# Attention scores of a hybrid transformer layer: the low parts of the queries on 128 rows

## The chip, the cores and the metric

One Trainium2 chip, one core. The metric is the time of one execution in microseconds on the device, the median of the runs. Engines are named as in the profile: PE is TensorE (PEld its weight loads), DVE is VectorE, ACT is ScalarE, POOL is GpSimd, SP issues DMAs.

## What is computed

One layer of a diffusion backbone in float32, for 512 latent tokens and 128 prompt tokens with the same weights: a modulated norm, one input projection to pooling channels, queries, keys, values and gates, a pooling mixer, a differential attention, gates and output projection, and a feed-forward part. The part that the change touches is the attention. Per head (8 of them) there are two maps m of 64 features; the latent queries read 640 keys (128 cached, 512 own), the prompt's queries read the 128 prompt keys:

```
def block(qi):
    s = jnp.einsum('bqhmd,bkhmd->bhmqk', qi, k).astype(jnp.float32) * scale
    p = jax.nn.softmax(s, axis=-1)
    a = p[:, :, 0] - lam * p[:, :, 1]
    return jnp.einsum('bhqk,bkhe->bqhe', a, vf)
```

## The kernel before

TensorE multiplies in a float32 format with a shortened mantissa. To keep the accuracy, every operand is split into a high part (the rounded value) and a low part (the rest), and a product is the sum of high x high, high x low and low x high, accumulated in PSUM. `mm` (L141) issues each of these products; all have line L142 in the profile, transposes L145.

The kernel runs in stages: startup (norm, modulation, the first head's projections), attention from about 78 to 382 us, pooling mixer and gates, output projection, feed-forward. In the attention the order on TensorE is written out by hand: `PHASES` (L465) has one string of steps per head, and `pin` (L136) keeps the program's order on TensorE. The order on VectorE, ScalarE and POOL is the planner's, which runs its own timing of the program (L1192). The steps are:

- `S`tm: `attend` (L651), scores of query tile t, map m: four products into one PSUM buffer `s`, then the maximum (`nm`, VectorE, L667), the exponential (`p`, ScalarE, L669), and after map 1 the scaled difference of both maps. For t = 4, the prompt's, both maps come at once with 128 keys each.
- `x`: `between` (L580), transposes of the cached keys of the next head and the prompt's new keys (`mx`), and sums of squares.
- `T`, `P`: `turned` (L679) transposes the differences (`pat`), `values` (L701) multiplies them with the values (`po`).
- `p`, `b`: one step of the projections that run between: queries (`psq`), keys (`psk`), values (`psv`), pooling channels (`psu`).

`s`, `pat` and `mx` share two PSUM buffers (`bankS`, L97), so the third of them in a row waits until the first one's readers are done.

The two maps lie on partitions 0 to 63 and 64 to 127. `k_split` writes, per map, a tile of 128 rows `ks`: the keys' high parts on the map's own rows, their low parts on the other 64. `q_part` (L552) writes, per map, `qd` with the queries' high part on both halves, and one tile `ql` for both maps with the low parts, each map's on its own rows (L562, VectorE); `ql` has two buffers, for the heads in turn. A score is then two products (`scores`, L645): `qd` with all 128 rows of `ks` (high x high and high x low at once), and the map's 64 rows of `ql` with its 64 rows of `ks` (low x high). The rotation of queries and keys (`rope`) runs on ScalarE, VectorE and POOL (L541), and POOL issues the stores of the new keys (L596) and values (L639).

The program is made in L1184 with the default size of the scratch that POOL's DMAs use, 16384 bytes per partition.

Of the kernel before, what the change touches and what calls it, by code (L numbers as in the profile page):

```python
# [12 lines left out]
F32R = mybir.dt.float32r  # L13
# [5 lines left out]
P = 128  # L19
# [48 lines left out]
def trunk_kernel(ctx: ExitStack, tc: tile.TileContext, a: dict, o: list):  # L68
# [46 lines left out]

    # ---------------------------------------------------------------- weights
    def wload(src, shape, name, eng=nc.vector):
        """src: DRAM AP of the tile's shape [P, a, b]; returns its exact (hi, lo) parts."""
        n = shape[0] * shape[1]
        raw = wpool.tile([P, 1024], F32, tag="raw", name=f"raw_{name}", bufs=3)  # L120
        rv = raw[:, :n]
        nc.sync.dma_start(rv.rearrange("p (a b) -> p a b", a=shape[0]), src)
        hi = wpool.tile([P, 1024], F32R, tag="whi", name=f"whi_{name}")
        lo = wpool.tile([P, 1024], F32R, tag="wlo", name=f"wlo_{name}")
        nc.scalar.copy(hi[:, :n], rv)  # L125
        eng.tensor_tensor(lo[:, :n], rv, f(hi[:, :n]), ALU.subtract)  # L126
        return (hi[:, :n].rearrange("p (a b) -> p a b", a=shape[0]),
                lo[:, :n].rearrange("p (a b) -> p a b", a=shape[0]))
# [7 lines left out]
    def pin(ins):  # L136
        """While pinned, the order on TensorE is the program's."""
        if pinned[0]:
            tc.keep_in_program_order(ins)
# [12 lines left out]
    def proj(ps, w, act, nk, c0=0, halves=(0, 1)):  # L152
        """ps[128 features, 640 tokens] = w[:, :, c0:c0+128]^T act, for these halves of the tokens."""
        (wh, wl), (ah, al) = w, act
        for k in range(nk):
            for i, (s, m) in enumerate(((wh, ah), (wh, al), (wl, ah))):
                for b in halves:
                    mm(ps[:, b, :HALF], s[:, k, c0:c0 + P], m[:, k, b * HALF:(b + 1) * HALF],
                       k == 0 and i == 0, k == nk - 1 and i == 2)
# [10 lines left out]

    # -------------------------------------------------------------- constants
    ident = const.tile([P, P], F32, tag="ident", name="ident")
# [20 lines left out]

    # ------------------------------------------------------------ modulation
    def put_shift(dst, ps, js):
# [12 lines left out]
    def ada_acc(pool, col, hf, name):  # L208
        """Generator: acc[p, cond, n] = sum over k of silu(c)[cond, k, p] * w_ada[k, p, col + n], with b_ada
        on partition 0, so that the sum over partitions is the modulation row."""  # L210
        c0 = col + hf * 512
# [20 lines left out]
    def acc_rows(acc, i, ps):  # L232
        """The rows of both conditions as rows 2 i and 2 i + 1 of ps[8, 512], i = 0 ... 3."""
        for n, x in enumerate(acc_split(acc, f"n2{i}")):
            for c in range(2):
                r = 2 * i + c
                mm(ps[:8, :], onerow[:, 7 - r:15 - r], x[:, c, :], i + n + c == 0, i + n + c == 5)

    def rows_cols(pool, ps):
        """Their columns: rows 0-3 are the shifts of norm 2 (two halves, two conditions), rows 4-7 the scales."""  # L240
        rows = pool.tile([8, 512], F32, tag="n2rows", name="n2rows", bufs=1)
# [11 lines left out]
    def acc_bcast(acc, dst, cols, name):  # L253
        """dst[c][128, cols] = the row on all partitions."""
        hi, lo = acc_split(acc, name)
# [13 lines left out]

    # ---------------------------------------------------------------- startup  # L270
    with tc.tile_pool(name="boot", bufs=1, reuse_waits="tile") as boot:
# [33 lines left out]
        def w_load(i):  # L305
            """Input rows i * 512 ... of the first head's q and k columns (0, 1); the second head's q columns (2)."""
            raw = wraw[i] = wpool.tile([P, 1024], F32, tag="raw", name=f"raw_first{i}", bufs=3)
# [76 lines left out]
        def ada_sum(i):  # L384
            """w_ada as the moving operand: in two exact parts, or (the first chunk) in float32 passes."""
            i, u = divmod(i, 10)
# [45 lines left out]
        def part(j, k):  # L432
            """Input rows k * 128 ... of the first head's queries (0), its keys (1), the second head's queries (2)."""
            if k == 0:
# [15 lines left out]

    # -------------------------------------------------------------- attention
    oraw = res.tile([P, NH, TOK], F32, tag="r2", name="oraw")
# [52 lines left out]
    with tc.tile_pool(name="att", bufs=2, reuse_waits="tile") as att:  # L505
# [4 lines left out]
        def cache_load(kind, i):  # L510
            """Cached keys or values of heads 2i and 2i + 1."""
            src, dst, n = {"ck": (cache_k, CK, 2), "cv": (cache_v, CV, 1)}[kind]
            dst[i] = att.tile([P, 256], F32, tag=kind, name=f"{kind}{i}", bufs=n)
            nc.sync.dma_start(dst[i], src[:, i * 256:(i + 1) * 256])
# [19 lines left out]
        def rope(ps, name, scale):  # L534
            """The positions' turn of the latent tokens, and a power of two as scale."""
            sh = att.tile([P, TOK], F32, tag="rsh", name=f"rsh_{name}")[:, :LAT]
# [15 lines left out]
        def q_part(h, ps=None, bank=bankP):  # L552
# [5 lines left out]
            qd = [att.tile([P, TOK], F32R, tag=f"qd{m}", name=f"qd{m}_{h}") for m in range(2)]  # L558
            ql = att.tile([P, TOK], F32R, tag="ql", name=f"ql{h}")
            for r, o, t in MAPS(qd):  # L560
                nc.scalar.copy(t[r], y[r])
                nc.vector.tensor_tensor(ql[r], y[r], f(t[r]), ALU.subtract)  # L562
                nc.gpsimd.tensor_copy(t[o], f(t[r]))
            Q[h] = qd, ql

        def MAPS(pair):
            """Per map: its rows, the others, its tile."""
            lo, hi = slice(0, HD), slice(HD, P)
# [5 lines left out]
        def k_split(h, y, cols):  # L574
            """High parts on the map's own rows, low parts on the others."""
            for r, o, t in MAPS(K[h]):
# [3 lines left out]
        def between(h, bank=bankS):  # L580
            """Cached keys of head h + 1, the prompt's new keys of head h, sums of squares of head h - 2: row r
            (tokens below HALF) and row 32 + r (the others) of ssq are head r's."""
            ps = bank(f"mx{h}")
# [61 lines left out]
        def scores(out, h, m, q0, k0, n):  # L645
            qd, ql = Q[h]
            r, _, k = MAPS(K[h])[m]
            mm(out, qd[m][:, q0:q0 + P], k[:, k0:k0 + n], True, False)
            mm(out, ql[r, q0:q0 + P], k[r, k0:k0 + n], False, True)

        def attend(h, t, m):  # L651
            """Map m of one query tile (t == 4: the prompt's, both maps); at the end, p0 / z0 - lam * p1 / z1."""
            name = f"{h}{t}"
# [25 lines left out]
        def turned(h, i):  # L679
            """The differences of key tiles 2i and 2i + 1, keys on partitions."""  # L680
            k0 = 2 * i
# [19 lines left out]
        def values(h, i):  # L701
            """Key tiles 2i and 2i + 1 of head h; the last call ends the head."""
            vh, vl = V[h // 2]
# [37 lines left out]
        def u_pool(g):  # L741
            """In place: the windows' means minus u itself, at u's own columns."""
            u = U[g]
# [28 lines left out]
        def weights(kind, i):  # L772
            """The weights of this step; those of the next one start to load."""
            n = need.index((kind, i))
# [11 lines left out]
        def project(b, n):  # L786
            """n steps of the projections that stand by."""
            while n:
# [5 lines left out]
        def step(h, op):  # L794
# [13 lines left out]
            else:  # L808
                between(NH + 1 if kind == "z" else h)

        W["q", 1] = FIRST[2]
        weights("q", 1)
# [29 lines left out]

    # ------------------------------------- pooling mixer, gates, merged branch
    with ExitStack() as mctx:
# [121 lines left out]

    # --------------------------------------------- output projection, norm 2
    h2 = mg
# [4 lines left out]
    def ffn_half(i, u):  # L973
        """Activation (u = 0) or gate tile i for the first half of the tokens; its PSUM tile and weights."""
        w = wcols(w_fi, u * FF + i * P, P, 0, KD, f"f{'au'[u]}{i}")
# [15 lines left out]
    with tc.tile_pool(name="wo", bufs=1, reuse_waits="tile") as wo:  # L991
# [16 lines left out]
        def out_steps(t):  # L1008
            """The output projection of tile t, then its residual and norm; yields after every second k."""
            ts = slice(t * P, (t + 1) * P)  # L1010
# [52 lines left out]

    # -------------------------------------------------------------------- ffn
    actx.close()
# [31 lines left out]
    def finish(t, pieces):  # L1097
        """The last columns of x2[t], from these PSUM pieces, and its norm: columns 0 to 511 are times fw already."""
        zs, c0 = [], 512
# [96 lines left out]
```

## Time and profile before

| | us |
|---|---|
| time, median of 3 runs | 1147.55 |
| lowest and highest | 1144.93, 1147.86 |
| profiled execution: span from the first to the last instruction | 1142.9 |
| profiled execution: TensorE busy | 1118.8 |
| profiled execution: VectorE busy | 695.0 |

The profiled execution has no time of its own beside the span; the table's median takes in what lies before the first instruction and after the last. An engine is counted as busy from an instruction's start to its end; products on TensorE overlap, so that their pace is read from the distance of their starts, not from their durations. An idle time that ended in "issue" is one in which the engine waited for nothing that the profile shows.

### The profile page before, as it was taken

The numbers are of one execution on the slowest core, as the hardware profiler recorded it, in microseconds if no ns is written. First come the engines' busy times: TensorE is split into PE (matmuls) and PEld (weight loads), VectorE is DVE, ScalarE is ACT, GpSimd is POOL, SyncE is SP. The second block draws the span as 40 slices with busy tenths as digits, with TensorE's granted clock in tenths as the row PEclk, the third lists the DMA queues.
The fourth block names the chain that finished last, engine by engine and source line by source line (L and its number), as shares of the span: only waits on it lengthen the run. The fifth ranks groups of instructions, "written<-read, shape, count | busy, mean of one in ns | idle before, by whom it ended". The sixth has DMA issues, their size and how long they took to land.

```text
span 1142.9 us, 16737 instructions
## 1 busy us (share of the span) xinstructions
PE 1118.8 (98%) x6811; PEld 1013.6 (89%) x6811; DVE 695.0 (61%) x1041; ACT 488.5 (43%) x783; POOL 158.6 (14%) x156
## 2 busy tenths in 40 slices
PE   6989999999999999999999999999999999999997
PEld 4778888888888999999999889999988899999886
DVE  5977767767775667787775658565424344444254
ACT  8746656656655454223233434333321133333123
POOL 3444223133121263000000000000000000000020
PEclk9989999999999999999999999999999999999999
DMA  9821112102101113446457105333222322222212
GB/s 310 234 72 60 48 30 63 38 26 80 38 23 41 37 56 117 142 149 184 149 164 238 60 19 148 91 113 92 73 85 69 89 74 75 74 75 78 70 38 92
DMA packets 128478, 106.10 MB, mean 93 GB/s; under 512 B 4173, under 2 KB 110205, under 8 KB 128402
## 3 DMA queue, kind: packets, MB, share of 16 engines
q1 hardware_dynamic: 126450, 101.93, 29.1%
q0 software_dynamic: 1232, 1.80, 0.7%
q8 instruction: 53, 0.87, 0.3%
q10 hardware_dynamic: 720, 1.31, 0.3%
q14 instruction: 23, 0.19, 0.1%
HBM read 101.36 MB, written 3.67 MB: 92 GB/s over the span
## 4 chain that ended last, share of the span: by engine, by line
PE 92%; DVE 3%; ACT 1%; SPq 1%; issue 1%; DMA 1%; ACTq 0%; DVEq 0%
PE pfa L142 13%; PE pfu L142 13%; PE acc L142 12%; PE ps_g L142 10%; PE s L142 7%; PE psyb L142 5%; PE psk L142 5%; PE pso L142 5%; PE psv L142 5%; PE psq L142 4%; PE psu L142 3%; PE po L142 3%; PE psya L142 2%; PE pat L145 2%; DMA araw_sh<-in_w_ada_dram 1%
## 5 line engine op out<-in xcount | busy, mean ns | idle before, releaser
L142 PE MATMUL pfu<-mg,whi_fu 128*128 128x320 f32 x704 | 134.1, 309 | 0.0
L142 PE MATMUL pfa<-mg,whi_fa 128*128 128x320 f32 x704 | 134.1, 309 | 0.0
L142 PEld LDWEIGHTS pfa<-mg,whi_fa 128*128 128x128 f32 x704 | 111.0, 188 | 0.4
L142 PEld LDWEIGHTS pfu<-mg,whi_fu 128*128 128x128 f32 x704 | 110.8, 188 | 0.0
L142 PE MATMUL acc<-whi_fo,gA 128*128 128x512 f32 (+1 forms) x336 | 101.0, 380 | 0.0
L142 PE MATMUL ps_g<-hT,whi_g 128*128 128x320 f32 x512 | 96.7, 311 | 0.0
L667 DVE TENSOR_REDUCE nm<-s 128x1 f32<-128x640 f32 (+1 forms) x80 | 57.2, 715 | 51.3 <-PE s L142 50.2
L669 ACT ACTIVATE p<-s,nm 128x640 f32<-128x640 f32 (+1 forms) x80 | 56.7, 709 | 61.0 <-DVE nm L667 60.4
L142 PE MATMUL pfa<-mg,wlo_fa 128*128 128x320 f32 x352 | 82.2, 307 | 0.0
L142 PE MATMUL pfu<-mg,wlo_fu 128*128 128x320 f32 x352 | 82.2, 307 | 0.0
L142 PEld LDWEIGHTS ps_g<-hT,whi_g 128*128 128x128 f32 x512 | 80.2, 188 | 2.0 <-issue 1.5
L126 DVE TENSOR_TENSOR wlo_fo<-raw_fo,whi_fo 128x1024 fp32r<-128x1024 f32 (+1 forms) x24 | 27.3, 1144 | 80.8 <-ACT whi_fo L125 80.8
L142 PEld LDWEIGHTS acc<-whi_fo,gA 128*128 128x128 f32 x336 | 62.1, 188 | 12.0
L142 PE MATMUL psv<-whi_v,hT 128*128 128x256 f32 x320 | 68.9, 296 | 0.3 <-DVE ks L578 0.3
L126 DVE TENSOR_TENSOR wlo_fa<-raw_fa,whi_fa 128x1024 fp32r<-128x1024 f32 x22 | 26.9, 1223 | 66.3 <-ACT whi_fa L125 66.3
L1171 POOL TENSOR_TENSOR x<-x,fw 128x512 f32<-128x512 f32 x5 | 6.9, 1370 | 419.0 <-ACT sq L1170 419.0
L125 ACT CAST whi_fo<-raw_fo 128x1024 fp32r<-128x1024 f32 (+1 forms) x24 | 23.3, 979 | 96.3 <-PE acc L142 71.3
L142 PE MATMUL acc<-wlo_fo,gA 128*128 128x512 f32 (+1 forms) x168 | 63.7, 380 | 0.0
L142 PEld LDWEIGHTS pfu<-mg,wlo_fu 128*128 128x128 f32 x352 | 59.4, 188 | 0.0
L142 PEld LDWEIGHTS pfa<-mg,wlo_fa 128*128 128x128 f32 x352 | 59.4, 188 | 0.0
L221 DVE SCALAR_TENSOR_TENSOR acc_g<-raw_g,silu,acc_g 128x512 f32<-128x512 f32 x64 | 44.5, 745 | 24.6 <-DMA raw_g<-in_w_ada_dram 24.6
L125 ACT CAST whi_fa<-raw_fa 128x1024 fp32r<-128x1024 f32 x22 | 23.1, 1052 | 84.7 <-PE pfa L142 61.7
(336 smaller groups left out, 2581.4 us busy)
## 6 DMA issues: line engine op xcount, KB each, us to landing
raw_fa<-in_w_ffn_in_dram SPq DMA_DIRECT2D x22, 512.0 KB
raw_fu<-in_w_ffn_in_dram SPq DMA_DIRECT2D x22, 512.0 KB
raw_fo<-in_w_ffn_out_dram SPq DMA_DIRECT2D x20, 512.0 KB
raw_g<-in_w_in_dram SPq DMA_DIRECT2D x16, 512.0 KB
raw_g<-in_w_ada_dram SPq DMA_DIRECT2D x16, 512.0 KB
araw_sh<-in_w_ada_dram SPq DMA_DIRECT2D x8, 512.0 KB
araw_sc<-in_w_ada_dram SPq DMA_DIRECT2D x8, 512.0 KB
raw_v<-in_w_in_dram SPq DMA_DIRECT2D x8, 512.0 KB
```

The costliest lines, as they stand in the source:

```text
L125: nc.scalar.copy(hi[:, :n], rv)
L126: eng.tensor_tensor(lo[:, :n], rv, f(hi[:, :n]), ALU.subtract)
L142: pin(nc.tensor.matmul(out, s, m, start=start, stop=stop))
L145: pin(nc.tensor.transpose(out, x, ident))
L221: nc.vector.scalar_tensor_tensor(acc[:, c, :], raw[:, ki, :], sc[:, c, 2 * u + ki:2 * u + ki + 1], acc[:, c, :], ALU.mult, ALU.add)
L667: nc.vector.tensor_reduce(nm[:, i:i + 1], s, AX.XY, ALU.max, negate=True)
L669: nc.scalar.activation(p.rearrange("p (b n) -> p b n", b=s.shape[1]), s, AF.Exp, bias=nm[:, i:i + 1], accum_out=z[:, i:i + 1])
L1171: nc.gpsimd.tensor_tensor(x2[t][:, hs], x2[t][:, hs], fw[:, hs], ALU.mult)
```

## The change

Each map gets its own tile of low parts with 128 rows, whose other 64 rows are zero, and the second product of a score runs over all 128 rows of that tile and of `ks`. Two pairs of these tiles are allocated once ahead of the attention and filled with zeros on the other rows by POOL; the heads take the pairs in turn. The scratch for POOL's DMAs goes from 16384 to 8192 bytes per partition. Comments and docstrings are dropped, too, which changes no instruction.

```diff
@@ -556,15 +556,15 @@  (q_part)
             qd = [att.tile([P, TOK], F32R, tag=f"qd{m}", name=f"qd{m}_{h}") for m in range(2)]
-            ql = att.tile([P, TOK], F32R, tag="ql", name=f"ql{h}")
-            for r, o, t in MAPS(qd):
+            ql = QL[h % 2]
+            for (r, o, t), (_, _, l) in zip(MAPS(qd), MAPS(ql)):
                 nc.scalar.copy(t[r], y[r])
-                nc.vector.tensor_tensor(ql[r], y[r], f(t[r]), ALU.subtract)
+                nc.vector.tensor_tensor(l[r], y[r], f(t[r]), ALU.subtract)
                 nc.gpsimd.tensor_copy(t[o], f(t[r]))
             Q[h] = qd, ql
@@ -644,12 +644,12 @@
         def scores(out, h, m, q0, k0, n):
             qd, ql = Q[h]
-            r, _, k = MAPS(K[h])[m]
+            k = K[h][m]
             mm(out, qd[m][:, q0:q0 + P], k[:, k0:k0 + n], True, False)
-            mm(out, ql[r, q0:q0 + P], k[r, k0:k0 + n], False, True)
+            mm(out, ql[m][:, q0:q0 + P], k[:, k0:k0 + n], False, True)
@@ -808,6 +808,11 @@
+        QL = [[att.tile([P, TOK], F32R, tag=f"ql{i}{m}", name=f"ql{i}{m}", bufs=1) for m in range(2)] for i in range(2)]
+        for pair in QL:
+            for _, o, t in MAPS(pair):
+                nc.gpsimd.memset(f(t[o]), 0.0)
         W["q", 1] = FIRST[2]
         weights("q", 1)
@@ -1181,7 +1186,8 @@
-    nc = _bacc.Bacc("TRN2", target_bir_lowering=False, num_devices=1)
+    nc = _bacc.Bacc("TRN2", target_bir_lowering=False, num_devices=1,
+                     dynamic_dma_scratch_size=8192)
```

## Rows read from the trace of the kernel before

**Rows 1.** The page: span, busy time, share of the span, instructions.

```profile
span 1142.9 us, 16737 instructions
...
PE 1118.8 (98%) x6811; PEld 1013.6 (89%) x6811; DVE 695.0 (61%) x1041; ACT 488.5 (43%) x783; POOL 158.6 (14%) x156
```

**Rows 2.** Stretches of 10 us: busy by engine (instructions), PEclk, DMA share, GB/s.

```profile
88.00:98.00 10.00, 10.00 (x57) 8.04 (x56) 5.40 (x10) 4.74 (x10) 3.09 (x3) 0.99 0.06 21
98.00:108.00 10.00, 10.00 (x58) 7.83 (x57) 8.54 (x15) 7.45 (x16) 4.17 (x2) 1.00 0.17 53
...
328.00:338.00 10.00, 10.00 (x66) 8.77 (x66) 9.54 (x16) 6.26 (x12) 2.54 (x3) 1.00 0.19 54
...
378.00:388.00 10.00, 10.00 (x61) 8.86 (x60) 7.45 (x26) 5.08 (x13) 1.25 (x1) 1.00 0.18 52
sum 300.00, PE 299.47 PEld 250.58 DVE 214.88 ACT 177.70 POOL 74.83; mean PE 9.98 PEld 8.35 DVE 7.16 ACT 5.92 POOL 2.49
```

**Rows 3.** PE's waits, 88 to 383 us: total us, times, longest us.

```profile
PE mx L145 <- ACT p L669: 0.4, 1, 0.4
```

**Rows 4.** Tile `s`: ns min/median/max, first and last start us, rows*columns of weights.

```profile
L142 PE MATMUL s<-ks,qd x144: 222/392/634, 78.7 to 381.2; 128*128 128x320 f32 x128, 128*128 128x128 f32 x16
...
L142 PE MATMUL s<-ks,ql x144: 322/410/633, 79.3 to 381.5; 64*128 64x320 f32 x128, 64*128 64x128 f32 x16
```

**Rows 5.** Timeline, one score group: start us, us, what [idle before].

```profile
228.50 0.28 PE L142 MATMUL psv<-whi_v,hT 128*128 128x256 f32 x1
228.50 0.19 PEld L142 LDWEIGHTS s<-ks,qd 128*128 128x128 f32 x1
228.62 0.31 PE L142 MATMUL s<-ks,qd 128*128 128x320 f32 x1
...
228.85 0.18 PEld L142 LDWEIGHTS s<-ks,ql 64*128 64x128 f32 x1 [0.16 <-issue]
...
229.19 0.19 PEld L142 LDWEIGHTS s<-ks,qd 128*128 128x128 f32 x1 [0.15 <-issue]
...
229.53 0.18 PEld L142 LDWEIGHTS s<-ks,ql 64*128 64x128 f32 x1 [0.16 <-issue]
...
229.87 0.19 PEld L142 LDWEIGHTS psv<-whi_v,hT 128*128 128x128 f32 x1 [0.15 <-issue]
```

**Rows 6.** Timeline of PE: six projection products, and the next.

```profile
226.14 0.75 PE L142 MATMUL psq<-hT,whi_q 128*128 128x320 f32 x4
...
227.02 0.75 PE L142 MATMUL psq<-hT,whi_q 128*128 128x320 f32 x4
```

**Rows 7.** Timeline of PE at the first two groups.

```profile
78.72 0.61 PE L142 MATMUL s<-ks,qd 128*128 128x320 f32 x1 [4.39 <-DVE ks L578]
...
81.24 0.60 PE L142 MATMUL s<-ks,qd 128*128 128x320 f32 x1 [0.23 <-DVE ks L578]
...
83.47 0.58 PE L142 MATMUL psv<-whi_v,hT 128*128 128x256 f32 x1
```

**Rows 8.** The stretch from 78 to 88 us, columns as in rows 2.

```profile
78.00:88.00 10.00, 9.05 (x27) 6.69 (x27) 7.02 (x10) 4.99 (x9) 3.58 (x3) 0.50 0.00 0
```

**Rows 9.** Timeline of PE, a group of the prompt, 128 columns.

```profile
224.24 0.22 PE L142 MATMUL s<-ks,qd 128*128 128x128 f32 x1
...
225.15 0.85 PE L142 MATMUL psq<-hT,whi_q 128*128 128x320 f32 x4
```

**Rows 10.** POOL by line: count, busy us, mean ns, idle before.

```profile
L596 POOL DMA_DIRECT2D out_dram<-nk x8 | 4.5, 565 | 27.1 <-ACT ks L577 20.5 <-ACT nk L595 6.6
L735 POOL MEMSET u<- 128x672 f32 x4 | 2.5, 660 | 2.1 <-PE s L142 2.1
```

**Rows 11.** Timeline of POOL ahead of the first head's rotation.

```profile
66.54 1.30 POOL L541 TENSOR_TENSOR ry_q<-ry_q,cos 128x512 f32<-128x512 f32 x1 [7.36 <-DVE rsh_q L540]
```

**Rows 12.** The page's part 3, POOL's DMA queue: packets, MB, share.

```profile
q0 software_dynamic: 1232, 1.80, 0.7%
```

## Prediction

> **What bounds the kernel now.** I read the page first: TensorE is busy 98% of a span of 1142.9 us, VectorE 61% [rows 1]. That says that TensorE sets the time as a whole, but a busy TensorE need not run at its pace, and the change touches one stage only, the attention from 78 to 382 us. So I read that stage in stretches of ten microseconds: in the 30 stretches from 88 to 388 us TensorE is busy 299.5 of 300 us and VectorE 214.9, from 5.4 to 9.5 of ten in the ones shown [rows 2]. The waits of TensorE from 88 to 383 us hold nothing longer than 0.4 us [rows 3]. So here TensorE's own pace sets the time, in an order that the program pins, and VectorE is the next engine, with no room in some stretches.
>
> Then I looked for TensorE not running at its pace while it counts as busy. The products of a score have two forms: the high product with 128 rows, the low product with 64, 144 of each, in 72 groups of four: 64 of 320 columns, 8 (the prompt's) of 128 columns [rows 4]. One group in order of time [rows 5]: the weights of the first high product are loaded at 228.50, before its predecessor's product has ended, and its product starts at 228.62. The next four loads start only at 228.85, 229.19, 229.53 and 229.87, each together with its product, each after an idle time of 0.15 or 0.16 us that ended on no wait ("issue"). The group takes 229.87 - 228.62 = 1.25 us for four products. Products of the same 320 columns that all contract 128 rows come six in 227.02 - 226.14 = 0.88 us, 0.147 us each [rows 6]. So at each border between a 128-row and a 64-row product, in both directions and also towards the next work behind the group, the weights' load is not drawn ahead, and the load and the refill lie open.
>
> **The change part by part.** *Low products on 128 rows.* The number of products, their columns and the loads' width stay; the rows that are added are zeros. If the border of row counts is what opens the gaps, each group goes at the pace of its neighbours: 4 x 0.147 = 0.59 us, so a group of 320 columns gives back 1.25 - 0.59 = 0.66 us. 62 such groups lie at full clock: 62 x 0.66 = 40.9 us. The first two lie in a stretch where the granted clock is 0.50, after a wait of 4.39 us [rows 7, 8]. The second took 83.47 - 81.24 = 2.23 us; at twice 0.147 us a product it takes 1.18: 1.0 us back. The first gives nothing, because the second waits for the same keys until 81.24. A group of 128 columns took 225.15 - 224.24 = 0.91 us [rows 9]. Full-row products of 128 columns have no run of their own to be read; the nearest are those of 256 columns ahead of the group, whose starts lie 228.62 - 228.50 = 0.12 us from the next one's [rows 5]; I take 0.12, four 0.48, 0.43 us back, 8 x 0.43 = 3.4. Sum: 40.9 + 1.0 + 3.4 = 45.3 us of TensorE.
>
> By the Trainium skill this sum would be empty: "TensorE: Matmul & The Clock Gate", Part 3, "The mechanism", says that a weights' load overlaps running products only when the row groups differ, so equal full rows would not overlap at all. The trace disagrees with it: the full-row load at 228.50 starts together with the full-row product ahead of it, of 0.28 us, and so overlaps it [rows 5].
>
> *What takes some of it back.* The softmax work of a group (maximum, exponential, scaling, difference) and the splits of queries, keys and values stay as long as they are, and TensorE's order only has two PSUM buffers for the tiles s, pat and mx, so TensorE can't run ahead of VectorE and ScalarE by more than that. 45.3 us over 300 is 1.5 per ten, so TensorE would want 8.5 us where it had 10. VectorE needs its busy time and about 0.03 us between two instructions. In 88 to 98 us it needs 5.40 + 10 x 0.03 = 5.7 and hinders nothing; in 98 to 108 us 8.54 + 15 x 0.03 = 9.0, an excess of 0.5; in 328 to 338 us 9.54 + 16 x 0.03 = 10.0, an excess of 1.5 [rows 2]. Summed over the 30 stretches of that view, from which the first, the last and two others stand, 12 exceed, by 10.6 us together. The length of the stretch is my choice: it says for how long work can be put off. With 20 us the same sum gives 2.7, with 5 us 17.3. Two buffers put off little, about two groups with their projections between (5 to 10 us), so I take the middle of 10.6 and 17.3: 14.0. Net: 45.3 - 14.0 = 31.3 us. Ends: 45.3 - 2.7 = 42.6 and 45.3 - 17.3 = 28.0.
>
> *The low parts' tiles.* VectorE's two subtractions per head keep their size, 64 rows by 640; they write to two tiles in place of one, two pairs in turn as before (two buffers). No wait is added once the zeros are in.
>
> *Four fills with zero on POOL, once.* Nearest row: a fill of 128 x 672 took 0.66 us; four of 64 x 640 are 2.6 us at most [rows 10]. They stand ahead of the first head's rotation on POOL, and before that rotation POOL is idle for 7.36 us [rows 11], which hides them: 0. They have to wait until the startup's tiles in that memory are read. Should that be late, or the planner place them later, what is queued behind on POOL is the rotation of the first head's queries and keys, and TensorE waits for just these keys (4.39 us [rows 7]): up to 2.6 us. Below nothing: no reason for a gain.
>
> *Halved scratch for POOL's DMAs, and other addresses.* Nothing in the rows shows a wait for the scratch. POOL issues a store of new keys in 0.565 us, and the queue moves 1232 packets in the whole run, 0.7% of the engines' time [rows 10, 12]. I take 0. If an issue had to wait, the 8 stores of keys would hold up POOL's rotations behind them; twice the issue time is 8 x 0.57 = 4.5 us more on an engine that is busy a quarter of the stage [rows 2], so little of it would reach TensorE. The order on VectorE, ScalarE and POOL isn't pinned and may come out differently; no row has a price for this.
>
> Sum against the profiled execution: 1142.9 - 31.3 = 1111.6 us of span. The median of the runs, 1147.55, lies 4.65 above that span; I keep this distance: 1116.2 us.
>
> **The rivals.** *The row count is not the cause.* The gaps could belong to score products as such: their moving operand, or two products on one accumulator. Then all stays: 1147.5 us. Against it: high products within the group, with the full 128 rows, suffer the same 0.34 us as low ones, and the first product of another kind behind the group too, while the first high product, behind full rows, is loaded ahead [rows 5]. Only the change of rows is common to these. Chance 4%, and it fills "no change" alone. By the rule of the Trainium skill's page above it would come out in this way.
>
> *VectorE gives back nothing or little.* If work is put off for longer than I think, up to 42.6 us: 1105 us or less, 5%.
>
> *TensorE's clock falls.* In the wait of 4.39 us ahead of the first group the granted clock went from 1.00 to 0.50 and stayed there for the whole stretch from 78 to 88 us [rows 7, 8]; that is 2.4 and 1.2 GHz, and such a stretch costs 10 x 0.5 = 5 us. Today no later wait of the stage reaches 0.4 us [rows 3]. The waits that are given back could gather into a few long ones, at the ends of heads where the prompt's group, the next head's first group and the cached keys follow each other with little between. One fall: 1121; two: 1126; three to six, 1131 to 1146, 7%. From the seventh on (7 x 5 = 35 > 31.3) the kernel is slower: with one in each of the eight heads 1147.55 - 31.3 + 40 = 1156 us. For it speaks that VectorE has no room in 12 stretches; against it, that 14 us of waits cannot make eight waits of the length seen. Chance of slower 3%.
>
> **How the numbers follow.** Forecast 1116 us, with 81% for the stretch around it. The upper end adds what is unknown to the small gain: 28.0 less one clock fall (5) less uncovered fills (2.6) leaves 20.4, 1127 us; the lower end is 1147.55 - 42.6 = 1105. The range 1105 to 1127 leaves out 5% below, 7% between 1127 and 1144, 4% at no change and 3% above. About 0.3% (3.4 us) is what a measurement of this kernel can tell from no change: faster 81 + 5 + 7 = 93%, same 4%, slower 3%.
>
> **What would show each step.** Right: the low products stand as 128*128, a group's four products start 0.147 us apart, and the load behind a group is drawn ahead; the idle time "issue" before score loads is gone. The span from the first group to the end of the pooling projections is some 31 us shorter, and every stage behind it keeps its length. TensorE's waits in the stage, 0.4 us now at most, add up to some 14 us, released by the exponential of an earlier group (its bank) or by VectorE's splits, mostly where VectorE was above 8.5 of ten. VectorE's busy time in the stage stays near 215 us. Wrong: gaps of 0.34 us that stay at full rows; a first group later than 78.7 us by a POOL queue of fills; a granted clock of 0.50 behind 90 us; POOL's store issues much longer than 0.57 us.

## The result, and the profile after

| | before | after |
|---|---|---|
| time, median (lowest to highest) | 1146.97 (1144.93 to 1147.86) | 1106.26 (1104.32 to 1108.31) |
| ratio of the times, 95% interval | | 0.9651 (0.9632 to 0.9669) |
| profiled execution: span | 1142.9 | 1106.5 |

The median of before takes in a fourth run, of 1146.38 us, beside the three of the prediction. The kernel is 40.7 us faster by the medians, 36.4 us by the two profiled executions. The forecast was 1116 us with a range of 1105 to 1127. The page of after, to be read against [rows 1]:

```profile
span 1106.5 us, 16752 instructions
...
PE 1071.1 (97%) x6811; PEld 1006.3 (91%) x6811; DVE 701.2 (63%) x1041; ACT 486.5 (44%) x783; POOL 163.0 (15%) x160
```

TensorE has the same 6811 products and is busy 47.7 us less, VectorE has the same 1041 instructions. The tile `s` answers [rows 4]: the low products now stand with 128 rows, and take 0.308 us in the median instead of 0.410.

```profile
L142 PE MATMUL s<-ks,qd x144: 219/310/604, 86.5 to 345.2; 128*128 128x320 f32 x128, 128*128 128x128 f32 x16
...
L142 PE MATMUL s<-ks,ql x144: 273/308/468, 86.9 to 345.4; 128*128 128x320 f32 x128, 128*128 128x128 f32 x16
```

One group in the timeline, as in [rows 5] (start, duration, engine, operation):

```profile
226.00 0.19 PEld L142 LDWEIGHTS s<-ks,qd 128*128 128x128 f32 x1
226.12 0.31 PE L142 MATMUL s<-ks,qd 128*128 128x320 f32 x1
226.12 0.19 PEld L142 LDWEIGHTS s<-ks,ql 128*128 128x128 f32 x1
...
226.27 0.19 PEld L142 LDWEIGHTS s<-ks,qd 128*128 128x128 f32 x1
...
226.42 0.19 PEld L142 LDWEIGHTS s<-ks,ql 128*128 128x128 f32 x1
...
226.57 0.19 PEld L142 LDWEIGHTS psv<-whi_v,hT 128*128 128x128 f32 x1
226.71 0.28 PE L142 MATMUL psv<-whi_v,hT 128*128 128x256 f32 x1
```

Every load now starts together with the product ahead of its own, and none has an idle time of "issue". The group takes 226.71 - 226.12 = 0.59 us, where it took 1.25.

Where the time went shows in one stretch: from the first score product to the first product of the gates (`ps_g`), before, then after. The columns are those of [rows 2]; TensorE's waits are the stretch less PE's busy time.

```profile
78.70:401.70 323.00, 322.22 (x1867) 270.29 (x1868) 229.20 (x389) 186.67 (x363) 85.15 (x78) 0.99 0.14 43
```

```profile
86.40:365.40 279.00, 270.10 (x1867) 259.38 (x1868) 232.58 (x388) 183.74 (x362) 85.97 (x77) 0.99 0.17 50
```

The attention stage shrank from 323.0 to 279.0 us with the same 1867 products; the waits went from 0.8 to 8.9. It begins 7.7 us later (86.4, 78.7), and behind it nothing changed (741.2 us before, 741.1 after). So 36.4 = 44.0 - 7.7 + 0.1. The waits, against [rows 3]:

```profile
PE mx L145 <- ACT p L669: 3.3, 3, 1.5
PE pat L145 <- ACT p L669: 1.5, 1, 1.5
PE s L142 <- ACT p L669: 1.3, 2, 0.9
PE s L142 <- DVE tl L693: 1.3, 1, 1.3
PE s L142 <- DVE ks L578: 0.6, 1, 0.6
PE s L142 <- issue: 0.4, 1, 0.4
...
```

Two more of 0.3 us are left out. Most end on the exponential of an earlier group, whose bank the next tile needs; the exponential itself waits for VectorE's maximum. By kinds of product, the distances from each start to the next in that stretch, waits taken out, sum up to this (some groups follow each other directly, so that 72 groups have 65 products behind them; last digits can be off by one through rounding):

| us, from the first score to `ps_g` | before | after | difference |
|---|---|---|---|
| score products of 320 columns (64 groups) | 83.6 | 40.2 | -43.4 |
| score products of 128 columns (8 groups) | 7.6 | 3.4 | -4.2 |
| the first product of another kind behind a group (65) | 16.0 | 9.9 | -6.1 |
| all other products | 215.1 | 216.6 | +1.6 |
| waits of TensorE | 0.8 | 8.8 | +8.1 |

What makes the other products 1.6 us longer wasn't followed.

### The profile page after: what moved, and what is told of

It reads as the page before. It is cut to its first block, busy times and chain, and to the rows that moved or that the text cites. A ratio compares the mean times of both kernels' runs of the same rounds, so it can differ in the third digit from the quotient of the medians.

```text
span 1106.5 us, 16752 instructions
## 1 busy us (share of the span) xinstructions
PE 1071.1 (97%) x6811; PEld 1006.3 (91%) x6811; DVE 701.2 (63%) x1041; ACT 486.5 (44%) x783; POOL 163.0 (15%) x160
## 4 chain that ended last, share of the span: by engine, by line
PE 80%; DVE 11%; ACT 4%; issue 2%; SPq 1%; DMA 1%; ACTq 0%; DVEq 0%
PE pfa L142 14%; PE pfu L142 14%; PE acc L142 13%; PE ps_g L142 10%; PE psyb L142 5%; PE pso L142 5%; PE psk L142 3%; PE psu L142 3%; PE psya L142 3%; PE s L142 2%; PE po L142 2%; PE psq L142 2%; DVE nm L667 2%; PE psv L142 2%; PE pat L145 1%
## 5 line engine op out<-in xcount | busy, mean ns | idle before, releaser
L142 PE MATMUL psv<-whi_v,hT 128*128 128x256 f32 x320 | 66.4, 288 | 0.0
```

Source lines behind the costliest of these rows:

```text
L142: pin(nc.tensor.matmul(out, s, m, start=start, stop=stop))
```

## The experiments

In each, "stage" is this same stretch, and a run's time lies 1.7 or 1.8 us above its span. The kernel before has a stage of 323.0 us and waits of 0.8; the kernel after 279.0 and 8.9.

**e1_scratch: the small scratch alone.** The kernel before with one argument added; the order of instructions on every engine is the same as before.

```diff
-    nc = _bacc.Bacc("TRN2", target_bir_lowering=False, num_devices=1)
+    nc = _bacc.Bacc("TRN2", target_bir_lowering=False, num_devices=1, dynamic_dma_scratch_size=8192)
```

> The kernel before with nothing but the scratch of POOL's DMAs at 8192 bytes. Theory (the gain comes from the 128-row products alone, the scratch is worth nothing): within 3.4 us of 1147, score groups of 1.25 us, the first group near 78.7 us. Rival (the halved scratch, the addresses or the order that the planner makes of them have a price or a gain of their own): below 1143.5, or above 1150.5 with a first group as late as the 86.5 us of the kernel after.

Measured: 1149.02 us in one run beside 1144.72 to 1149.3 for the kernel before; stage 322.9. The scratch does nothing in the stage. But the first group came at 83.18 instead of 78.72, with the startup's clock lower than in the profile of before. The stretch from 50 to 60 us in before, then in this run:

```profile
50.00:60.00 10.00, 10.00 (x66) 9.30 (x67) 8.40 (x17) 3.88 (x7) 4.18 (x4) 1.00 0.91 180
```

```profile
50.00:60.00 10.00, 8.98 (x40) 7.80 (x38) 8.39 (x17) 3.95 (x7) 4.09 (x7) 0.66 0.80 149
```

The seventh value is the granted clock: 1.00, and a mean of 0.66, so a part of the stretch at the lower level (1.2 GHz); TensorE got 40 products started where it had 66. Whether the scratch causes that was left to e7 and e8.

**e2_low64: the new tiles, fills and scratch, but the low products on 64 rows.**

```diff
-            k = K[h][m]
+            r, _, k = MAPS(K[h])[m]
...
-            mm(out, ql[m][:, q0:q0 + P], k[:, k0:k0 + n], False, True)
+            mm(out, ql[m][r, q0:q0 + P], k[r, k0:k0 + n], False, True)
```

> The kernel after with everything of the change but the rows: two tiles of low parts per head, the four fills with zero and the small scratch stay, but the second product of a score again takes the map's own 64 rows. Theory (borders between 128 and 64 rows are the whole gain): score groups are back at 1.25 us, and the time is that of the kernel before plus the late start of the attention seen after the change (7.7 us): 1147 to 1155. Rival (tiles, scratch or the planner's order brought the gain): well below 1147, near 1106 if all of it.

Measured: 1149.45 us, stage 323.2:

```profile
L142 PE MATMUL s<-ks,qd x144: 219/392/634, 83.3 to 386.0; 128*128 128x320 f32 x128, 128*128 128x128 f32 x16
L142 PE MATMUL s<-ks,ql x144: 323/410/633, 83.9 to 386.2; 64*128 64x320 f32 x128, 64*128 64x128 f32 x16
```

With 64 rows both forms have the medians of before again, 0.392 and 0.410 us; the high products too, which this edit leaves alone. The rows of the second product are the whole gain, and nothing else in the change has a part in it.

**e3_hhll: the kernel before, each group ordered high, high, low, low.** The products stay as they are; only the borders between 128 and 64 rows go from four to two in a group.

```diff
...
+            for out, m, q0, k0, n in todo:
+                mm(out, qd[m][:, q0:q0 + P], K[h][m][:, k0:k0 + n], True, False)
+            for out, m, q0, k0, n in todo:
+                r, _, k = MAPS(K[h])[m]
+                mm(out, ql[r, q0:q0 + P], k[r, k0:k0 + n], False, True)
...
```

> The kernel before with one thing changed: the four products of a score group stand as high, high, low, low in place of high, low, high, low, so that a group has two borders (into the 64 rows and out of them) in place of four. Theory (each border costs): starts in the group some 0.15, 0.24, 0.15 and 0.34 us apart, sum 0.88 in place of 1.25; 64 x 0.37 = 24 us less work for TensorE, time 1123 to 1128 as far as VectorE lets it through. If low after low on the same 64 rows isn't drawn ahead, 0.25 in place of 0.15 and some 1130. Rival (the cost sticks to the low product or to score products as such): the sum stays near 1.25 and the time within 3.4 us of 1147.

Measured: 1116.62 us, stage 294.9, waits 1.7, score products 62.3 us instead of 91.2. A group, and one of the prompt:

```profile
169.34 0.46 PE L142 MATMUL s<-ks,qd 128*128 128x320 f32 x2
169.72 0.29 PEld L142 LDWEIGHTS s<-ks,ql 64*128 64x128 f32 x2 [0.19 <-issue]
...
170.20 0.19 PEld L142 LDWEIGHTS psv<-whi_v,hT 128*128 128x128 f32 x1 [0.19 <-issue]
...
174.86 0.33 PE L142 MATMUL s<-ks,qd 128*128 128x128 f32 x2
175.12 0.18 PEld L142 LDWEIGHTS s<-ks,ql 64*128 64x128 f32 x2
175.12 0.33 PE L142 MATMUL s<-ks,ql 64*128 64x128 f32 x2
175.38 0.19 PEld L142 LDWEIGHTS psv<-whi_v,hT 128*128 128x128 f32 x1
```

The group takes 170.20 - 169.34 = 0.86 us, for 1.25 in [rows 5] and 0.59 in after: with half of the borders, the same products in number, size and rows give back more than half of the difference. So it is the border that costs. The expected split within the group was off, though: taken singly, the four starts and the next lie 0.146, 0.239, 0.252 and 0.232 us apart in this group. The 0.252 between the two low products isn't a load that stays behind. Seen by itself, the second one's load starts at 169.83, ahead of its own product at 169.97, while at a border load and product start together:

```profile
169.83 0.19 PEld L142 LDWEIGHTS s<-ks,ql 64*128 64x128 f32 x1
```

The 0.252 is the second half of a border's price: the product behind a border delays the one that follows it by 0.10 us, here a low one. In before, the first product behind a group starts together with its load at 229.87 [rows 5], and the next of its kind 0.22 us later, where 0.12 is their pace:

```profile
230.09 0.28 PE L142 MATMUL psv<-wlo_v,hT 128*128 128x256 f32 x1
```

In e3 that distance is 0.22, too. Counted so, the four borders of before cost 0.66 + 0.10 = 0.76 us and the two of e3 0.86 - 0.59 + 0.10 = 0.37, that is 0.19 each in both. The time lies below the expected 1123 to 1128: the stage is 28.1 us shorter, since the groups of 320 columns gave 25.7 (24 expected), the prompt's groups, which the expectation left out, 3.2, and the waits rose by 0.9 only.

**e4_early_zeros: the kernel after, its zero fills moved to the start.** The tiles get memory of their own, and the fills are pinned behind POOL's first DMA issues; the change's fills ahead of the attention go.

```diff
+    zq = zctx.enter_context(tc.tile_pool(name="zq", bufs=1, reuse_waits="tile"))
+    QL = [[zq.tile([P, TOK], F32R, tag=f"ql{i}{m}", name=f"ql{i}{m}") for m in range(2)] for i in range(2)]
...
+        for pair in QL:
+            for o, t in zip((slice(HD, P), slice(0, HD)), pair):
+                pin(nc.gpsimd.memset(f(t[o]), 0.0))
```

> The kernel after, with the four tiles of low parts in a pool of their own that lies beside the startup's memory, and the four fills pinned on POOL right behind its DMA issues of the startup (about 10 us) in place of ahead of the first head's rotation (50.7 us). Theory A (the fills and what they push back on POOL, the broadcasts of lambda and the last low part of the activations, delay the first head's keys): the first score group comes back from 86.5 to 79 to 81 us and the time to 1099 to 1102. Theory B (the late start comes from the granted clock, which fell twice in the startup of the profiled execution, and from the projections of the values that the planner put ahead of the last key products): the first group stays where these two leave it, 83 to 87 us, and the time stays within 1103 to 1109.

Measured: 1101.26 us (1100.76 to 1102.18), ratio to before 0.9597 (0.9576 to 0.9619). The stage is that of after (279.4 us), the start that of before; the order of instructions on TensorE, VectorE and ScalarE is again the one of before:

```profile
79.00 0.60 PE L142 MATMUL s<-ks,qd 128*128 128x320 f32 x1 [4.39 <-DVE ks L584]
```

The first group comes at 79.00, behind the same wait of 4.39 us as in [rows 7].

**e5_less_dve: the kernel after with less on VectorE.** The weighted sum of both maps (L677, 40 instructions) is left out, so that the second map is missing in the output.

```diff
-                nc.vector.scalar_tensor_tensor(A[h, t], A[h, t], z[:, 0:1], p, ALU.mult, ALU.add)
```

> The kernel after without VectorE's weighted sum of the two maps (38 operations of 0.79 us between 88 and 383 us, some 30 us of VectorE): the first map's exponentials go on alone, so the second map is left out of the output. Read is the attention stage, from the first score product to the first gate product (278.95 us after the change, with 8.8 us of TensorE's waits in it). Theory (the waits are VectorE being late): by the sums over stretches of the trace of before, with this work taken out, the waits fall to 4 us or less and the stage to 271 to 275 us. Rival (they are the latency from a score to the exponential that frees its bank, with VectorE not late): waits stay at 7 to 9 us and the stage at 277 to 279.

**e6_more_dve: the kernel after with more on VectorE.** The maximum of each second map is taken once more, into a tile that nobody reads (40 instructions, 28.2 us).

```diff
+                if i:
+                    nx = att.tile([P, 1], F32, tag="nx", name=f"nx_{name}", bufs=4)
+                    nc.vector.tensor_reduce(nx, s, AX.XY, ALU.max, negate=True)
```

> The kernel after with the maximum of every second map's scores taken twice, the second one into a tile that nobody reads: 40 operations more, some 28 us of VectorE (32 of 0.82 us and 8 of 0.27). Theory (VectorE is the next bound and has no room left): the sums over stretches of the trace of before rise by 19 to 21 us, so the stage goes from 279 to some 298 us. Rival (VectorE still has room, and TensorE's order alone sets the stage): 279 to 285 us.

Measured: 1099.24 us with less and 1127.55 us with more. The stages, e5's first:

```profile
82.10:356.30 274.20, 270.21 (x1867) 260.16 (x1868) 200.34 (x348) 183.73 (x362) 86.51 (x77) 0.99 0.17 50
```

```profile
83.50:384.40 300.90, 275.72 (x1867) 262.37 (x1868) 257.12 (x428) 183.19 (x362) 88.14 (x77) 0.98 0.16 46
```

| VectorE busy in the stage | waits of TensorE | stage |
|---|---|---|
| 200.3 of 274.2 (e5) | 4.0 | 274.2 |
| 232.6 of 279.0 (after) | 8.9 | 279.0 |
| 257.1 of 300.9 (e6) | 25.2 | 300.9 |

32 us less on VectorE take 4.8 us from the stage, 25 us more add 21.9. VectorE's load thus sets most of the waits, and it is the next bound: taking a seventh of its work away leaves 4.0 us of waits, and what is added to it now is mostly paid. Neither run changes VectorE's load alone, since the planner's order on VectorE and ScalarE moved in places with it; TensorE's order stayed. Of e6's 21.9 us, 25.2 - 8.9 = 16.3 are waits and 275.7 - 270.1 = 5.6 are busy time, at a clock of 0.98 in place of 0.99. Of its waits, the first line has no releaser in the profile, but each of its six ends 0.1 us behind an exponential; none ends on the added maximum, which reads the score buffer, too:

```profile
PE s L142 <- issue: 8.7, 6, 2.7
PE pat L145 <- ACT p L672: 6.2, 5, 2.9
PE s L142 <- DVE ks L578: 4.4, 2, 3.1
PE s L142 <- ACT p L672: 4.0, 6, 1.2
```

**e7_scratch_again and e8_before_again: is the startup's clock the scratch's doing?** The kernel of e1 in three rounds, and the kernel before once more with a profile.

> The kernel before with the small scratch once more, its instructions in the same order on every engine, now with several timed runs. Theory (its late first group, 83.2 us against 78.7, came from the granted clock that fell in the startup of that one execution, which the kernel before does too in some executions): the median is within 3.4 us of the kernel before's, and runs without a fall take 1144 to 1146 us. Rival (the shifted addresses bring these falls): every run of it 1147 or more, and the median 2 to 4 us above the kernel before's.

> The kernel before unchanged, for a second profile of its startup. Theory (the clock's falls in the startup come and go between executions of one program): with a time of 1147 or more this profile shows one or two falls to 0.50 between 30 and 60 us and a first group at 80 to 84 us; with a time near 1145 none and 78.7 us. In both cases the time is the span plus 1.8 us, as in all profiled executions whose time is known. Rival (the kernel before never falls there): no fall and a first group at 78.7 us with a time above 1147.

Measured: 1147.59 us (10 runs, 1144.46 to 1149.07) against 1146.08 for before on the same chip (13 runs, 1144.58 to 1148.8), ratio 1.001 (0.9995 to 1.0025): no difference. e8 took 1144.55 us with its first group at 78.46. Both kernels show the same times again and again, about 1144.6, 1146.3, 1147.4 (before only) and 1148.9. e1 and e7 are one program, with its first group at 83.18 and 80.12 us. One program thus has starts of different length, and the profile of before (span 1142.9, so 1144.7 us) was one of its shortest executions.

**e9_values_pool: e4 with the split of the value weights on POOL.** If VectorE is the next bound, less on it should be worth something without leaving work out.

```diff
-            return [wcols(w_in, COL_V + hp * 256, 256, 4 * i, 4, f"v{hp}{i}") for i in range(2)]
+            return [wcols(w_in, COL_V + hp * 256, 256, 4 * i, 4, f"v{hp}{i}", nc.gpsimd) for i in range(2)]
```

> The kernel of the early zeros, with the low parts of the values' weights (8 operations of 1.22 us on VectorE, two before each pair of heads) made on POOL. Theory (VectorE's full stretches cost TensorE some 9 us of waits, and taking away 30 us of VectorE gave back 5): a third of that work off VectorE gives 1 to 2 us: 1099 to 1101. Rival (on POOL such an operation takes 2.4 us and comes late for the first pair of heads, whose products start right behind the startup): the first score group moves from 79 us to 80 to 83 and the time to 1101 to 1105.

Measured: 1109.15 us (1107.16 to 1111.55), ratio 0.9682 (0.9657 to 0.9707), slower than e4's kernel on the same chip (1102.49, below). The first group came at 81.2 us, as the rival had it, but the time lies beyond both expectations. Its stage:

```profile
81.20:368.10 286.90, 272.05 (x1868) 260.48 (x1869) 231.23 (x385) 184.56 (x363) 102.96 (x84) 0.99 0.16 48
```

POOL has 16.5 us more than in e4 (86.5), VectorE only 2.2 less (233.4), and the waits went from 9.1 to 14.9. A split takes 2.4 us on POOL. The planner's order moved in places here, too. Which of its followers is late then, the rotation behind it on POOL or the values themselves, wasn't separated.

**e4b_early_zeros and e10_after_again: the start once more, side by side.** The kernels of e4 and after, on one chip.

> The kernel of the early zeros once more, on the same chip as the run before it, for the comparison: 1100.5 to 1102.5 us, the first score group near 79 us, no fall of the granted clock between 20 and 75 us in the profiled execution, the stage 279 to 280 us.

> The kernel after unchanged, beside the early zeros on the same chip. Theory (its startup is longer by the value products that the planner put ahead of the last key products, 1.5 us, and by the later chain to the first keys, 1.5 us, and the clock's falls come on top in most executions): best runs at 1104 to 1105, 3 us above the early zeros' best, median 1105 to 1107. Rival (the whole difference is the falls, which come and go): best runs near 1101.

Measured: e4's kernel 1102.49 us (1100.71 to 1104.39), ratio 0.9629 (0.9608 to 0.965); after 1104.7 us (1103.71 to 1108.48), ratio 0.9654 (0.9632 to 0.9676). The lowest times of both lie 3.0 us apart. The profile of e10 had full clock from 20 to 70 us, and is thus the start of after without the clock's share. The last key products of the first head and the first group, in before, e10 and after:

```profile
62.36 0.46 PE L142 MATMUL psk<-hT,wlo_first 128*128 128x320 f32 x2
```

```profile
64.17 0.46 PE L142 MATMUL psk<-hT,wlo_first 128*128 128x320 f32 x2
...
82.07 0.61 PE L142 MATMUL s<-ks,qd 128*128 128x320 f32 x1 [6.60 <-DVE ks L578]
```

```profile
68.26 0.46 PE L142 MATMUL psk<-hT,whi_first 128*128 128x320 f32 x2
68.55 0.46 PE L142 MATMUL psk<-hT,wlo_first 128*128 128x320 f32 x2
...
86.45 0.60 PE L142 MATMUL s<-ks,qd 128*128 128x320 f32 x1 [6.60 <-DVE ks L578]
```

So the 7.7 us of the start have two parts: 82.07 - 78.72 = 3.35 us that the program of after has at full clock, and 86.45 - 82.07 = 4.38 us that its profiled execution lost to the clock, in stretches of which this is one, to be held against e10's with 1.00:

```profile
50.00:60.00 10.00, 8.67 (x37) 7.53 (x36) 8.56 (x17) 4.04 (x8) 6.19 (x11) 0.66 0.81 159
```

## Why the prediction was right, and where its steps were not

*The mechanism was right.* The gaps belonged to the border between 128-row and 64-row products: e2 brings all of them back with the rows alone, e3 takes half of them away with the order alone. The rival that the row count isn't the cause is out, and with it the rule of the Trainium skill's page "TensorE: Matmul & The Clock Gate", Part 3, "The mechanism", as the prediction takes it: the loads of after overlap full-row products ahead of them, and e3's load at 169.83 overlaps a product on the same 64 rows. (The same section also has loads pulled ahead that go to a background weight buffer; that fits these rows.) What the runs show is closer to another page of the Trainium skill, "TensorEngine Tiling (Array Packing)", "Key Properties", by which a change of the tiling mode drains TensorE. It gives no price; here four borders cost 0.66 us in a group and 0.10 in the product behind it, 0.19 each.

*Gross, 45.3 us: too small.* The score products gave back 47.6 us. The groups of 320 columns gave 43.4 (forecast 40.9 + 1.0 = 41.9). The groups of 128 columns took 0.42 us, not the 0.48 that products of 256 columns suggested, and gave 4.2, not 3.4. And one term was missing: the first product behind a group paid for the border too, and those 65 products took 6.1 us less; all other products took 1.6 more. All products together: 47.6 + 6.1 - 1.6 = 52.1 us.

*Give-back by VectorE, 14.0 us: too large, 8.1 measured.* The kind was right: the waits end where the forecast put them, on an earlier group's exponential and on VectorE's splits, and e5 and e6 show that VectorE's load sets most of their sum. The step that failed is the sum itself, "12 exceed, by 10.6 us together". By the rule that stands there (busy time plus 0.03 us per instruction, against 8.5), only six of the 30 stretches exceed, by 4.4 us: two in [rows 2], by 0.5 and 1.5, and these four, by 0.8, 0.5, 0.1 and 1.0.

```profile
108.00:118.00 10.00, 10.00 (x62) 8.65 (x61) 8.76 (x17) 7.09 (x18) 3.51 (x3) 1.00 0.41 126
118.00:128.00 10.00, 10.00 (x59) 8.35 (x57) 8.65 (x12) 6.16 (x10) 3.36 (x3) 1.00 0.18 53
...
228.00:238.00 10.00, 10.00 (x67) 8.64 (x66) 8.11 (x15) 6.13 (x13) 5.40 (x4) 1.00 0.20 60
...
308.00:318.00 10.00, 10.00 (x61) 8.23 (x59) 8.96 (x18) 6.53 (x15) 2.48 (x3) 1.00 0.21 61
```

With 20 us the same rule gives 1.3, not 2.7, and with 5 us 10.3, not 17.3. The numbers of the prediction come out nearly (10.7 in 12 stretches, 2.7, 17.8) where the durations of VectorE's instructions are added up in place of its busy time: their records overlap, and the overlap counts twice. The middle of 4.4 and 10.3 is 7.3, near the 8.1 measured. That is one measurement of a rough rule: most of VectorE's records overlap the one before, so that few of them leave the 0.03 us, and without it the sums are 2.0 and 5.4. For how long work can be put off is therefore not shown. VectorE's busy time held (229.2 and 232.6 us in the stage).

*Fills and scratch, 0: right for POOL's time and for the scratch.* The four fills took 2.89 us, not "2.6 us at most", and ran in one of POOL's gaps ahead of the first rotation, where POOL is still idle for 10.93 us:

```profile
50.68 2.89 POOL L815 MEMSET ql<- 64x640 f32 x4
...
59.26 2.54 POOL L421 TENSOR_TENSOR hT<-xT,hT 128x640 fp32r<-128x640 f32 x1 [3.62 <-DVE xT L417]
72.73 1.30 POOL L541 TENSOR_TENSOR ry_q<-ry_q,cos 128x512 f32<-128x512 f32 x1 [10.93 <-DVE rsh_q L540]
```

A store of new keys still takes POOL 0.566 us (0.565 in [rows 10]).

*The planner's order, no price: 3.35 us.* This is the step that the prediction left without a term. The first head's group was to come no later than 78.7 us, and came 3.35 us later at full clock. The fills didn't stand in the way on POOL; the planner made another order of the new program. The profile of after has twelve value products (12 x 0.12 = 1.4 us) ahead of the first head's last key products, which before stood behind them. The way from these products' end to the first group also grew, from 78.72 - 62.82 = 15.9 us to 82.07 - 64.63 = 17.4 (e10; 86.45 - 69.01 = 17.4 in after). Its last steps on VectorE show where, in before and then in e10:

```profile
77.75 0.82 DVE L578 TENSOR_TENSOR ks<-ry_k,ks 64x640 fp32r<-64x640 f32 x1
78.60 1.64 DVE L542 TENSOR_TENSOR rsh_q<-rsh_q,sin 128x512 f32<-128x512 f32 x1
```

```profile
79.43 0.69 DVE L542 TENSOR_TENSOR rsh_q<-rsh_q,sin 128x512 f32<-128x512 f32 x1
80.15 1.77 DVE L578 TENSOR_TENSOR ks<-ry_k,ks 64x640 fp32r<-64x640 f32 x1
```

The key split `ks`, for which the first group waits, has changed places with a step of the next head's rotation: it starts 0.7 us later for that, and takes 1.77 us instead of 0.82. In both profiles the longer of the two is the one during which POOL runs a step of the same rotation (L541); that POOL is the reason isn't shown. e4, with the order of before, has 79.00 - 63.11 = 15.9 again, and its fastest runs are 3.0 us faster than those of after.

*The clock rival didn't decide.* Apart from its beginning, where before has one too [rows 8], the stage shows no fall of the clock; its mean is 0.99 before and after. It was the startup that lost 4.4 us in the profiled execution of after, and 4.5 us in e1, whose program has the order of before.

*The distance of 4.65 us.* It was taken for something that lies around every execution. It is 1.8 us; the rest was the start of other executions than the profiled one. Without this error the forecast would have been 1111.6 + 1.8 = 1113.4, nearer to the 1106.26.

*Luck.* 1106.26 lies 1.3 us above the lower end of the range. It lies in the range because of the late start, for which the sum has no term: e4, with the start of before, took 1101.3 and 1102.5 us, below 1105, and the second median of after itself, in e10, is 1104.7. With VectorE's sum and the distance put right the forecast would have been 1142.9 - 45.3 + 7.3 + 1.8 = 1106.7; that it would nearly hit is luck as well, since the 6.8 us that the gross lacks and the 7.7 us of the start cancel.

In one line, the two profiled executions: forecast -45.3 + 14.0 = -31.3; measured -52.1 + 8.1 + 7.7 - 0.1 = -36.4. Three terms were off by 6 to 8 us: the gross and the give-back to the one side, the start to the other.

*The better version.* e4's kernel, the change with its fills at the start, has medians of 1101.3 and 1102.5 us, faster than before, and in the comparison on one chip 2.2 us faster than after (1102.49 and 1104.7); the four runs of each overlap in their range.

## What to carry to other kernels

Read the pace of products from the distance of their starts, and look whether the next weights' load starts beside the product ahead: where operands of 128 and 64 rows alternate it doesn't, and rows of zeros, or an order with fewer borders, give the time back without a product less. A border's price shows in two places, ahead of the product behind it and in that product's own distance to the next. When TensorE becomes faster in a stage, sum the next engine's busy time over stretches of several lengths, not the durations of its instructions, which can overlap, and name the result as a range. An edit in a program whose order a planner makes can also move work in unpinned places: put setup work where it has a fixed place, at the start.

## What the runs showed of the hardware that was not expected

- Two products of 64 rows on different halves run side by side: in e3's prompt group they start 0.004 us apart, and both together last 0.33 us (the row at 175.12), as one alone does in the timeline of e2 below. The Trainium skill's "TensorE: Matmul & The Clock Gate", in its part "Why this matters for your kernels", gives up to 4 ns for products in different row groups; the trace agrees.

```profile
229.12 0.33 PE L142 MATMUL s<-ks,ql 64*128 64x128 f32 x1
```

- A border between 128 and 64 rows cost 0.19 us with products of 320 columns, in two parts: 0.09 before the product behind it starts (0.24 us in place of 0.147), and 0.10 before that product's follower starts (0.25 in place of 0.147 in e3, 0.22 in place of 0.12 behind a group). Between two products of 64 rows on the same half the load is drawn ahead (169.83 in e3).
- The same program has starts that differ through the clock granted to TensorE, from one execution to the next: by 4.4 us for after (its profile and e10), by 3.1 for the kernel of e1 and e7.
